# Sharing one pool between the operands of even head pairs and the first chunks' Gram operands, and loading the first of these during the operand stage

## The chip, the cores and the metric

The kernel runs on one core of one Trainium2 chip. The metric is the device time of one execution in microseconds (us); the lower the better. The kernel before was timed three times: 1175.95, 1177.39 and 1180.84 us, median 1177.39 us.

## The reference

A two-layer encoder trunk on x of 1024 positions by 1024 channels, float32. Layer 0: RMSNorm, one projection of 1024 to 4224 columns, mixer A (RWKV-7 time mixing, 8 heads of 64), mixer B (chunked attention, 8 heads of 64), gates, output projection, residual. Layer 1: RMSNorm, projection, gMLP spatial gating, output projection, residual; then a last RMSNorm. What matters here is mixer A's recurrence, which the kernel computes in chunks of 64 positions:

```
def step(state, inp):
    r_t, w_t, k_t, v_t, a_t, b_t = inp
    sa = einsum('bhvk,bhk->bhv', state, a_t)
    state = state * w_t + sa x b_t + v_t x k_t
    y_t = einsum('bhvk,bhk->bhv', state, r_t)
```

Here r, k and v are token-shifted slices of the projection, w the decay, a_t = -kk and b_t = kk * a.

## The kernel before

**Projections.** Every float32 matmul with the large weights is made as three fp32r products (high x high, high x low, low x high; lines 256, 258, 260). The tile they add into is named `acc`, and these matmuls are called acc matmuls below. 128 columns of weights are loaded by SyncE (`wraw`, line 221), split by ScalarE and GpSimd (`wh` line 222, `wl` line 225) and used in two halves of 24 acc matmuls.

**Operand stage** (lines 539 to 640). Four pairs of heads, `p` = 0 to 3, each with two halves of 512 positions. For each pair k, r and v are projected into the tiles `kT`, `rT`, `vT`, then `ar` (the a and r operands) and `bk` (the b and k operands) are formed and stored to DRAM: `ar_d` by line 604, `bk_d` by lines 535 and 537 in three stores. The function `bonus` stores v as `v_d` (line 626). `kT`, `rT` and `vT` are four halves each in the pools `rst` and `ra`, so that pairs p and p+2 use the same halves. These pools live on the left side of SBUF and are closed by `pi.close()` (line 640).

**Gram stage**, `stage_a(q)`, q = 0 to 3 (lines 667 to 728). A quarter has 4 chunks, taken in two chunk pairs `cg` = 0, 1. Per chunk pair SyncE loads `bk` (line 694, one load), `ag` (line 696, two loads, one for each head of a pair) and `uv` (line 699, four small loads). TensorE makes 16 Gram matmuls (line 713, `psg`; each shows as two instructions in the trace) in two groups of 8; VectorE masks each group out of PSUM into `G` and `ag` (line 717, four operations, with the mask `gmask` that GpSimd builds at line 656); GpSimd scales `bk` (line 678) and TensorE transposes it (line 684, `pst`). In the first quarter `bk` of cg 0 and both `ag` are tiles of the pool `re_`, which lies where `rst` and `ra` lay, and `bk` of cg 1 is a tile of `rb` on the right side.

**Inverse and recurrence.** `stage_b(q)` (line 730) inverts the unit triangular blocks: 30 short VectorE operations on `nq`, then ScalarE's `xe` (line 757), transposes to `dt`, and small matmuls `psx` (line 770). `stage_c(q)` (line 796) runs the four chunks in order, with matmuls `zz`, `yy`, `us` and copies `z`, `uv` between them; `zz` and `yy` of the first chunk stand among the Gram matmuls.

**Filling.** `Fill` hands out the acc matmuls of attention's projections between the small matmuls; their results leave by `split_evac` (`hl`, to `q_d` and `k_d`) and `vb_evac` (ScalarE's `vs`, line 893, then four transposes `pv`, line 896). The order on each engine is made by the Tile framework's scheduler from priorities and its own estimate of when each operand is ready; each engine then runs its row in order, and SyncE's row holds all DMA issues.

Of the kernel before, what the change touches and what calls it, by code (L numbers as in the profile page):

```python
# [8 lines left out]
F32 = mybir.dt.float32  # L9
# [9 lines left out]
P = 128  # L19
# [34 lines left out]
LATE = 1  # L54
NPO = 1
QP = 84
FILLS = [5, 4, 4, 6, 4, 3, 3, 3]
QA = 14
QB = [80, 10, 10, 10]
# [40 lines left out]
def trunk_kernel(  # L100
# [4 lines left out]
    nc = tc.nc  # L105
# [20 lines left out]
        (sg_ln_g.rearrange("a (r c) -> (a r) c", c=P), 8),  # L126
    ]
    nrow = sum(n for _, n in rows)
    pi = ExitStack()
    ca = pi.enter_context(tc.tile_pool(name="ca", bufs=1))  # L130
    rst = pi.enter_context(tc.tile_pool(name="rst", bufs=1, reuse_waits="tile"))
# [14 lines left out]
    o = 0  # L146
# [295 lines left out]
    def lora_evac(ps, hf):  # L442
# [5 lines left out]
            tc.add_manual_dep(i_.ins, evs[-1][0].ins.name, sched_only, reason="issue order")  # L448
        nc.vector.tensor_tensor(xw[64:128, sl], w, f32(xw[0:64, sl]), op=ALU.subtract)
        nc.vector.tensor_tensor(xa[0:64, sl], a, f32(xa[64:128, sl]), op=ALU.subtract)  # L450
    new_half = lambda tag: (rst if tag == "kT" else ra).tile([P, 512], F32, tag=tag, name=tag, bufs=4)
    kT = [new_half("kT") for _ in range(2)]
    sh_k = shifted(kT, 4)
    for hf in range(2):
        run(half_steps(w_lora, hf, lora_evac))
# [81 lines left out]
            nc.sync.dma_start(dst[64:128, :, 64 * i:64 * i + 64], src[64:128, :, 64 - 64 * i:128 - 64 * i])  # L537

    for p in range(NPAIR):
        rT, vT = ([new_half(tag) for _ in range(2)] for tag in ("rT", "vT"))  # L540
        if p > 0:
            kT = [new_half("kT") for _ in range(2)]
            proj_cm(w_in_e[0], 512 + p * P, shifted(kT, 4 + p))
        after = evs[AFW[0]][0] if p == 0 and AFW[0] else None
        proj_cm(w_in_e[0], p * P, shifted(rT, p), after=after)
# [118 lines left out]
    hss = [slice(64 * h, 64 * h + 64) for h in range(2)]  # L664
    oss = hss[::-1]

    def stage_a(q):

        d = quart[q]
        d["ag"], d["g"], d["bt"], d["uv"] = [], [], [], []  # L670
        rq = (re_, rb)[q % 2]
        parts = []

        def rest(cg, bk, bt):

            c0 = 4 * q + 2 * cg
            for i in range(2):
                nc.gpsimd.tensor_tensor(
                    bk[:, :, i, :], bk[:, :, i, :], pcs[:, c0 + i, :].unsqueeze(2).to_broadcast([P, 4, P]), op=ALU.mult)
            for pj in range(2):  # L680
                pst = ps_m.tile([P, 4, P], F32, tag="m", name="pst")
                for j in range(2):
                    for i in range(2):
                        nc.tensor.transpose(pst[:, 2 * j + i], bk[:, 2 * pj + j, i, :], ident)
                nc.scalar.copy(bt[:, 2 * pj:2 * pj + 2].rearrange("p j i t -> p (j i) t"), pst)

        for cg in range(2):
            o = 4 * q + 2 * cg
            uv = rq.tile([P, 2, 4, P], F32, tag="uv", name="uv", bufs=2)

            ag = rq.tile([P, 2, 4, 2, P], F32, tag="ag", name="ag", bufs=2)
            bk = (rb if q == 0 and cg else re_).tile(
                [P, 4, 2, P], F32, tag="bt" if q == 0 and cg else "bk", name="bk", bufs=2 if q == 0 and cg else 1)
            nc.sync.dma_start(bk, bk_d[o // 8][:, :, o % 8:o % 8 + 2, :].rearrange("a p c t -> p a c t"))
            for h in range(2):
                nc.sync.dma_start(ag[hss[h], h], ar_d[o // 8][:, hss[h], o % 8:o % 8 + 2, :].rearrange("a p c t -> p a c t"))
            for i in range(2):
                for h in range(2):
                    nc.sync.dma_start(
                        uv[oss[h], i, :, hss[h]],  # L700
                        v_d[o // 8][:, 64 * (o % 8 + i):64 * (o % 8 + i) + 64, hss[h]].rearrange("a s n -> s a n"))
                    if q == cg == i == 0:
                        nc.gpsimd.memset(uv[hss[h], i, :, hss[h]], 0.0)
            if cg == 0:
                d["G"] = rq.tile([P, 2, 4, 2, P], F32, tag="G", name="G", bufs=1)
            g = d["G"][:, cg]
            bt = rq.tile([P, 4, 2, P], F32, tag="bt", name="bt", bufs=2)
            for pj in range(2):
                psg = [ps_m.tile([P, 4, P], F32, tag="m", name=f"psg{h}") for h in range(2)]
                for j in range(2):  # L710
                    for i in range(2):
                        for h in range(2):
                            nc.tensor.matmul(psg[h][:, 2 * j + i], lhsT=bk[hss[h], 2 * pj + j, i, :],  # L713
                                             rhs=ag[hss[h], h, 2 * pj + j, i, :], start=True, stop=True)
                for h in range(2):
                    for dst, r in ((g[:, 2 * pj:2 * pj + 2], hss[h]), (ag[:, h, 2 * pj:2 * pj + 2], oss[h])):
                        nc.vector.tensor_tensor(
                            dst[r].rearrange("p j i t -> p (j i) t"), psg[h][r],
                            gmask[r].unsqueeze(1).to_broadcast([64, 4, P]), op=ALU.mult)
            d["g"].append(g)  # L720
            d["ag"].append(ag)
            d["bt"].append(bt)
            d["uv"].append(uv)
            parts.append((cg, bk, bt))
            if q > 0:
                rest(*parts.pop())
        for a in parts:
            rest(*a)
# [197 lines left out]
    for q in range(3):  # L926
# [4 lines left out]
        fill.pump(QB[q + 1], mark, FLB)  # L931
        stage_d(q)
    pe.close()


    pb = ExitStack()
# [450 lines left out]
```

## Time and profile before

| | |
|---|---|
| median of three runs | 1177.39 us (1175.95 to 1180.84) |
| profiled execution | 1180.27 us, of which the trace spans 1178.6 us |
| mean granted TensorE clock | 0.974 |
| TensorE busy | 1119.8 us, 95% of the span |
| VectorE, ScalarE, GpSimd busy | 53%, 40%, 37% |
| operand stage, Gram stage, recurrence | to about 265 us, from 269 us on, to about 545 us |

Engines are named as in the trace: PE = TensorE, PEld = its weight loads, DVE = VectorE, ACT = ScalarE, POOL = GpSimd, SP = SyncE. A timeline row gives the start, the time taken, engine, line, operation, tiles, count, and in square brackets the idle time ahead of it with what ended it. A row of the windows view gives the busy time and count of each engine in that stretch, then the clock granted to TensorE (1.00 is full), the busy share of the DMA engines and GB/s. All positions are us from the span's start.

### The profile page before, as it was taken

How to read it: one execution, taken by the hardware profiler on the slowest of the kernel's cores; microseconds unless marked ns; L12 is line 12 of the kernel's file. 1: busy time of each engine (PE TensorE's matmuls, PEld its weight loads, DVE VectorE, ACT ScalarE, POOL GpSimd, SP SyncE). 2: the span in 40 equal slices, each digit the busy share in tenths (PEclk: the TensorE clock that was granted, in tenths of full speed). 3: DMA queues.
4: the chain of work that ended last, by engine and by line, in shares of the span. 5: the costliest groups of instructions: out<-in, count | busy, mean ns of one | idle time of the engine just before them, and what ended most of it. 6: DMA issues, size and time to landing. Idle time of an engine off the chain costs nothing.

```text
span 1178.6 us, 21117 instructions
## 1 busy us (share of the span) xinstructions
PE 1119.8 (95%) x8162; PEld 929.2 (79%) x8162; DVE 622.6 (53%) x1276; ACT 469.0 (40%) x1008; POOL 432.0 (37%) x448
## 2 busy tenths in 40 slices
PE   8999999998899898999997899899999999999997
PEld 5788778787777676767886778789998888888886
DVE  6455656456585867634687767464100753333433
ACT  5554554430322232312675646234417232231432
POOL 4345545361223433423322463311402464351222
PEclk9999999995999998999999899999999999999999
DMA  6124446469322533293587784862401232122541
GB/s 209 39 81 143 116 117 164 140 205 193 109 83 83 161 101 100 73 215 118 162 227 184 222 264 147 270 216 90 134 10 55 87 110 72 63 88 89 166 133 71
DMA packets 169125, 156.39 MB, mean 133 GB/s; under 512 B 25257, under 2 KB 138562, under 8 KB 168898
## 3 DMA queue, kind: packets, MB, share of 16 engines
q1 hardware_dynamic: 169026, 155.06, 44.9%
q8 instruction: 64, 1.05, 0.4%
q14 instruction: 35, 0.29, 0.1%
HBM read 102.02 MB, written 53.00 MB: 132 GB/s over the span
## 4 chain that ended last, share of the span: by engine, by line
PE 58%; DMA 7%; DVE 5%; ACT 1%; issue 1%; POOL 1%; SPq 0%; DVEq 0%; ACTq 0%; POOLq 0%
PE acc L256 8%; PE acc L258 8%; PE acc L260 8%; PE accv L256 3%; PE accv L260 3%; PE accv L258 3%; PE accu L256 3%; PE accu L260 2%; PE accg L260 2%; PE accu L258 2%; PE accg L258 2%; PE accg L256 2%; PE st L1069 2%; DMA wraw<-in_w_out_e_dram 2%; PE psx L770 1%; PE psg L713 1%
## 5 line engine op out<-in xcount | busy, mean ns | idle before, releaser
L256 PE MATMUL acc<-xH,wh 128*128 128x512 f32 x528 | 214.7, 407 | 1.6 <-DVE rT L422 0.6
L258 PE MATMUL acc<-xL,wh 128*128 128x512 f32 x528 | 213.5, 405 | 0.0
L225 POOL TENSOR_TENSOR wl<-wraw,wh 128x512 fp32r<-128x512 f32 (+1 forms) x106 | 148.9, 1424 | 175.4 <-ACT wh L222 160.0
L260 PE MATMUL acc<-xH,wl 128*128 128x512 f32 x528 | 212.0, 401 | 0.0
L256 PEld LDWEIGHTS acc<-xH,wh 128*128 128x128 f32 x528 | 101.5, 192 | 23.6 <-DVE rT L422 1.0
L258 PEld LDWEIGHTS acc<-xL,wh 128*128 128x128 f32 x528 | 101.2, 192 | 21.2 <-issue 0.9
L260 PEld LDWEIGHTS acc<-xH,wl 128*128 128x128 f32 x528 | 101.0, 191 | 21.2
L256 PE MATMUL acc<-WHL,yh 128*128 128x512 f32 x256 | 101.9, 398 | 4.5 <-DVE res L1142 3.4
L222 ACT CAST wh<-wraw 128x512 fp32r<-128x512 f32 (+1 forms) x102 | 62.7, 653 | 108.5 <-PE acc L258 43.3
L258 PE MATMUL acc<-WHL,yh 128*128 128x512 f32 x256 | 100.8, 394 | 0.0
L260 PE MATMUL acc<-WHL,yl 128*128 128x512 f32 x256 | 100.8, 394 | 0.0
L256 PE MATMUL accv<-wh,xH 128*128 128x256 f32 x256 | 71.7, 283 | 0.0
L258 PE MATMUL accv<-wl,xH 128*128 128x256 f32 x256 | 71.7, 283 | 0.0
L260 PE MATMUL accv<-wh,xL 128*128 128x256 f32 x256 | 71.4, 285 | 0.0
L256 PEld LDWEIGHTS acc<-WHL,yh 128*128 128x128 f32 x256 | 48.4, 189 | 15.6 <-DVE res L1142 4.1
L258 PEld LDWEIGHTS acc<-WHL,yh 128*128 128x128 f32 x256 | 48.3, 189 | 9.6 <-POOL WHL L1114 0.2
L260 PEld LDWEIGHTS acc<-WHL,yl 128*128 128x128 f32 x256 | 48.1, 188 | 9.7
L256 PE MATMUL accu<-xH,wh 128*128 128x512 f32 x128 | 50.5, 395 | 0.0
L260 PE MATMUL accu<-xH,wl 128*128 128x512 f32 x128 | 49.9, 390 | 0.0
L258 PE MATMUL accu<-xL,wh 128*128 128x512 f32 x128 | 49.9, 390 | 0.0
L260 PE MATMUL accg<-xH,wl 128*128 128x512 f32 x128 | 49.9, 389 | 0.0
L256 PE MATMUL accg<-xH,wh 128*128 128x512 f32 x128 | 49.8, 389 | 0.0
(433 smaller groups left out, 2438.0 us busy)
## 6 DMA issues: line engine op xcount, KB each, us to landing
wraw<-in_w_in_e_dram SPq DMA_DIRECT2D x66, 256.0 KB
wraw<-in_w_in_o_dram SPq DMA_DIRECT2D x32, 256.0 KB
xt<-in_x_dram SPq DMA_DIRECT2D x8, 512.0 KB
ar_d<-ar SPq DMA_DIRECT2D x8, 512.0 KB
q_d<-hl SPq DMA_DIRECT2D x8, 512.0 KB
bk<-bk_d SPq DMA_DIRECT2D x8, 512.0 KB
ag<-ar_d SPq DMA_DIRECT2D x16, 256.0 KB
k_d<-hl SPq DMA_DIRECT2D x8, 512.0 KB
```

Of the source, the lines that this page charges most:

```text
L222: c_ = hi(wh[:, ks], raw)
L225: nc.gpsimd.tensor_tensor(wl[:, ks], raw, f32(wh[:, ks]), op=ALU.subtract)
L256: fill(nc.tensor.matmul(ps, lhsT=ah(k), rhs=bh(k), start=(k == 0), stop=False), k == 0)
L258: fill(nc.tensor.matmul(ps, lhsT=ah(k), rhs=bl(k), start=False, stop=False), False)
L260: fill(nc.tensor.matmul(ps, lhsT=al(k), rhs=bh(k), start=False, stop=(k == nk - 1)), False)
L713: nc.tensor.matmul(psg[h][:, 2 * j + i], lhsT=bk[hss[h], 2 * pj + j, i, :], rhs=ag[hss[h], h, 2 * pj + j, i, :], start=True, stop=True)
L770: nc.tensor.matmul(ps[t_, i], lhsT=lhsT(f, i), rhs=rhs[f[0], i], start=True, stop=True)
L1069: nc.tensor.transpose(st[:, o:o + P], pfs[j][:, k0:k0 + P], ident)
```

## The change

A new pool `eo` is opened ahead of the operand stage's pools and closed after the last `stage_d` of the loop. It has two tiles: `e4` of 4 KB and `e8` of 8 KB for each partition. `kT` of pairs 0 and 2 is now one `e4` tile, `rT` and `vT` of these pairs one `e8` tile; odd pairs keep `rst` and `ra`, with two halves of each kind where there were four. `ag` of the first chunk pair of quarters 0 and 2 is an `e8` tile, and every `bk` but that of quarter 0's second chunk pair is an `e4` tile. The first chunk pair's `bk` and `ag` loads get a priority 1000 steps higher.

```
+FIRST = 1000
+    es = ExitStack()
+    eo = es.enter_context(tc.tile_pool(name="eo", bufs=1, reuse_waits="tile"))
...
-    new_half = lambda tag: (rst if tag == "kT" else ra).tile([P, 512], F32, tag=tag, name=tag, bufs=4)
-    kT = [new_half("kT") for _ in range(2)]
+    def operands(p):
+
+        if p % 2:
+            return ([(rst if tag == "kT" else ra).tile([P, 512], F32, tag=tag, name=tag, bufs=2) for _ in range(2)]
+                    for tag in ("kT", "rT", "vT"))
+        k_ = eo.tile([P, 2, 512], F32, tag="e4", name="kT", bufs=1)
+        rv = eo.tile([P, 4, 512], F32, tag="e8", name="rvT", bufs=1)
+        return ([t_[:, i] for i in range(o, o + 2)] for t_, o in ((k_, 0), (rv, 0), (rv, 2)))
+
+    kT, rT, vT = operands(0)
...
     for p in range(NPAIR):
-        rT, vT = ([new_half(tag) for _ in range(2)] for tag in ("rT", "vT"))
         if p > 0:
-            kT = [new_half("kT") for _ in range(2)]
+            kT, rT, vT = operands(p)
...
-            ag = rq.tile([P, 2, 4, 2, P], F32, tag="ag", name="ag", bufs=2)
-            bk = (rb if q == 0 and cg else re_).tile(
-                [P, 4, 2, P], F32, tag="bt" if q == 0 and cg else "bk", name="bk", bufs=2 if q == 0 and cg else 1)
-            nc.sync.dma_start(bk, bk_d[o // 8][:, :, o % 8:o % 8 + 2, :].rearrange("a p c t -> p a c t"))
-            for h in range(2):
-                nc.sync.dma_start(ag[hss[h], h], ar_d[o // 8][:, hss[h], o % 8:o % 8 + 2, :].rearrange("a p c t -> p a c t"))
+            ap_, at_, ab_ = (eo, "e8", 1) if q % 2 == cg == 0 else (rq, "ag", 1 + q % 2)
+            ag = ap_.tile([P, 2, 4, 2, P], F32, tag=at_, name="ag", bufs=ab_)
+            bp_, bt_, bb_ = (rb, "bt", 2) if q == 0 and cg else (eo, "e4", 1)
+            bk = bp_.tile([P, 4, 2, P], F32, tag=bt_, name="bk", bufs=bb_)
+            with tc.high_priority(offset=FIRST if q == cg == 0 else 0):
+                nc.sync.dma_start(bk, bk_d[o // 8][:, :, o % 8:o % 8 + 2, :].rearrange("a p c t -> p a c t"))
+                for h in range(2):
+                    nc.sync.dma_start(
+                        ag[hss[h], h], ar_d[o // 8][:, hss[h], o % 8:o % 8 + 2, :].rearrange("a p c t -> p a c t"))
```

How the rows of the engines move is shown at three places. First SyncE's row before, from the stores of the last pair's first half on (line 604 stores `ar`, 537 and 535 store `bk`, 221 loads weights, 432 stores a gate):

```order
L604 DMA ar_d_109<-ar 128x1024
L432 DMA bg_d<-gt 128x512
L537 DMA bk_d_111<-bk 512x1x64
L535 DMA bk_d_111<-bk 64x1024
L537 DMA bk_d_111<-bk 512x1x64
L221 DMA wraw<-in_w_in_e_dram 128x4x128
L432 DMA bg_d<-gt 128x512
```

The same place in the change, where the numbers of lines and of DRAM tiles are a few higher (616 is 604, 548 and 550 are 535 and 537, 225 is 221; 710 and 708 load `ag` and `bk`):

```order
L616 DMA ar_d_112<-ar 128x1024
L436 DMA bg_d<-gt 128x512
L710 DMA ag<-ar_d_112 64x4x256 x2
L548 DMA bk_d_114<-bk 64x1024
L550 DMA bk_d_114<-bk 512x1x64 x2
L225 DMA wraw<-in_w_in_e_dram 128x4x128
L708 DMA bk<-bk_d_114 128x4x256
L436 DMA bg_d<-gt 128x512
```

The first chunk pair's three loads now stand behind the stores they read. Further on in SyncE's row, at the end of the operand stage, stood before:

```order
L221 DMA wraw<-in_w_in_e_dram 128x4x128
L694 DMA bk<-bk_d_111 128x4x256
L696 DMA ag<-ar_d_109 64x4x256 x2
L699 DMA uv<-v_d_113 64x4x64 x4
L694 DMA bk<-bk_d_111 128x4x256
L696 DMA ag<-ar_d_109 64x4x256 x2
```

and stands in the change (714 loads `uv`):

```order
L225 DMA wraw<-in_w_in_e_dram 128x4x128
L714 DMA uv<-v_d_116 64x4x64 x4
L708 DMA bk<-bk_d_114 128x4x256
L714 DMA uv<-v_d_116 64x4x64 x2
L710 DMA ag<-ar_d_112 64x4x256 x2
```

The second chunk pair's `ag` has seven small or large loads ahead of it since the weights, and had eight. Second, TensorE's row before, at the end of the last acc matmuls ahead of the Gram stage:

```order
L258 MATMUL acc<-xL,wh 128x512
L260 MATMUL acc<-xH,wl 128x512
L713 MATMUL psg_2566<-ag,bk 128x128 x4
L713 MATMUL psg_2567<-ag,bk 128x128 x4
L713 MATMUL psg_2580<-ag,bk 128x128 x4
L814 MATMUL zz<-uv,ag 64x64
L817 MATMUL yy<-uv,ag 64x64
L713 MATMUL psg_2581<-ag,bk 128x128 x4
```

and in the change (728 is 713), nineteen acc matmuls earlier:

```order
L260 MATMUL acc<-xH,wh 128x512
L262 MATMUL acc<-xL,wh 128x512
L728 MATMUL psg_2561<-ag,bk 128x128 x2
L728 MATMUL psg_2562<-ag,bk 128x128 x2
L728 MATMUL psg_2561<-ag,bk 128x128
L728 MATMUL psg_2562<-ag,bk 128x128
L728 MATMUL psg_2561<-ag,bk 128x128
L728 MATMUL psg_2562<-ag,bk 128x128
L264 MATMUL acc<-xH,wl 128x512
```

The first group of 8 has moved ahead of the last nineteen acc matmuls; the second group (now `psg_2575` and `psg_2576`) and the second chunk pair follow these, in the order they had. Third, ScalarE's row before, after the Gram stage (685 copies the transposed `bk`, 222 splits weights, 884 is the `hl` copy, 757 `xe`, 893 `vs`, 898 the copy of `pv`):

```order
L884 ACTIVATE hl<-acc 128x512
L685 COPY bt<-pst 128x512 x2
L757 ACTIVATE xe<-nq,half 128x16x16 x2
L893 ACTIVATE vs<-acc 128x512
L898 CAST vv<-pv 128x8x64
L222 CAST wh<-wraw 128x512 x2
```

and in the change (697 is 685, 772 is 757, 908 is 893, 913 is 898):

```order
L899 ACTIVATE hl<-acc 128x512
L697 COPY bt<-pst 128x512 x2
L908 ACTIVATE vs<-acc 128x512
L913 CAST vv<-pv 128x8x64
L772 ACTIVATE xe<-nq,half 128x16x16 x2
L226 CAST wh<-wraw 128x512 x2
```

`vs` and the copy of its transposes have changed places with `xe`. From here to the end of `stage_c(2)` the rows of TensorE, VectorE, ScalarE and GpSimd stand in another order at many places, with the same operations; from `stage_c(3)` on they stand almost as before.

More of the change, by code (lines that the diff above doesn't have):

```diff
@@ L933, in trunk_kernel @@
     pe.close()
+    es.close()
     pb = ExitStack()
```

## The prediction

> **What bounds the kernel now.** I read the page first: how much of the span TensorE is busy, and at what clock.
>
> ```profile
> PE 1119.8 (95%) x8162; PEld 929.2 (79%) x8162; DVE 622.6 (53%) x1276; ACT 469.0 (40%) x1008; POOL 432.0 (37%) x448
> ...
> PEclk9999999995999998999999899999999999999999
> ```
>
> TensorE is the bound: 95% busy, no other engine over 53%. So a change can win in two ways only: less idle time of TensorE, or a fuller clock while it is busy. The tenth slice of the clock shows 5 where the others show 8 or 9, and it lies at 265 to 295 us, where the Gram stage begins. So I took the windows view there, cut at the places where TensorE's work changes, and once over the stretch of inverse and recurrence.
>
> ```profile
> 265.40:269.20 3.80, 0.01 (x1) 0.00 (x0) 0.00 (x0) 0.00 (x0) 0.00 (x0) 1.00 1.15 257
> 269.20:285.70 16.50, 16.45 (x96) 14.68 (x96) 9.53 (x15) 0.00 (x0) 2.37 (x3) 0.53 1.16 215
> 285.70:288.80 3.10, 1.85 (x9) 1.47 (x9) 3.02 (x4) 0.59 (x1) 1.71 (x2) 0.50 0.61 175
> 288.80:294.00 5.20, 5.20 (x14) 4.12 (x13) 4.70 (x12) 0.65 (x2) 0.00 (x0) 0.50 0.31 101
> 300.60:304.00 3.40, 1.21 (x18) 1.01 (x18) 2.12 (x9) 1.39 (x3) 0.45 (x2) 1.00 0.57 172
> 304.00:307.70 3.70, 3.70 (x12) 3.03 (x13) 3.61 (x6) 0.59 (x1) 0.00 (x0) 0.54 0.01 2
> 330.00:545.00 215.00, 199.33 (x2996) 156.06 (x2995) 135.47 (x296) 60.13 (x127) 75.97 (x88) 0.96 0.44 121
> ```
>
> The first row is a hole of 3.8 us. In the next three rows, 25 us in all, TensorE is busy, but at half its clock. Then the same once more in small: a hole in 300.6 to 304.0, half clock behind it. The timeline of TensorE says what ends the holes.
>
> ```profile
> 264.79 0.39 PE L258 MATMUL acc<-xL,wh 128*128 128x512 f32 x1
> 265.02 0.39 PE L260 MATMUL acc<-xH,wl 128*128 128x512 f32 x1
> 269.25 4.93 PE L713 MATMUL psg<-ag,bk 64*128 64x128 f32 x24 [3.85 <-DMA ag<-ar_d]
> 277.37 2.07 PE L713 MATMUL psg<-ag,bk 64*128 64x128 f32 x8
> 282.62 3.09 PE L713 MATMUL psg<-ag,bk 64*128 64x128 f32 x16
> 300.55 1.17 PE L713 MATMUL psg<-ag,bk 64*128 64x128 f32 x16
> 303.91 0.82 PE L896 MATMUL pv<-ident,vs 128*128 128x128 f32 x4 [2.19 <-ACT vs L893]
> 378.65 1.16 PE L713 MATMUL psg<-ag,bk 64*128 64x128 f32 x8
> ```
>
> Acc matmuls start 0.23 us apart (first two rows). The first hole is ended by the load of `ag`, the second by ScalarE's `vs`. Gram matmuls at half clock take 2.07 us for 8 instructions; at full clock 1.16 us, or 1.17 us for 16 where the heads alternate. The first chunk pair runs from 269.25 to 277.37, the second from there to 285.71 (282.62 + 3.09), 8.3 us. Last, the issues of SyncE:
>
> ```profile
> 229.42 0.32 SPq L604 DMA_DIRECT2D ar_d<-ar  x1
> 233.74 0.52 SPq L537 DMA_DIRECT2D bk_d<-bk  x1
> 238.94 0.38 SPq L221 DMA_DIRECT2D wraw<-in_w_in_e_dram  x1
> 261.71 1.28 SPq L694 DMA_DIRECT2D bk<-bk_d  x1
> 263.04 1.37 SPq L696 DMA_DIRECT2D ag<-ar_d  x2
> 264.51 2.55 SPq L699 DMA_DIRECT2D uv<-v_d  x4
> 267.11 0.60 SPq L694 DMA_DIRECT2D bk<-bk_d  x1
> ```
>
> The first pair's data was stored from 229.4 and 233.7 us on, but its loads are issued at 261.7 to 264.4; the last lands 4.8 us after its issue.
>
> **Part by part.** I follow the new order with these durations, in the profiled execution's own time (1180.27 us, span 1178.6).
>
> *The early loads and the first group.* In the change the three loads stand behind the stores, so they land some 15 us before their use. The first 8 Gram matmuls come nineteen acc matmuls earlier: at 265.4 - 19 x 0.23 = 261.1 us. They take 1.2 us, and the nineteen acc matmuls end at 266.6 where they ended at 265.4: so the first group costs no wait. Its masking on VectorE needs `gmask`, and takes four operations:
>
> ```profile
> 261.66 0.92 POOL L656 TENSOR_SCALAR_AFFINE_SELECT gmask<-gmask 64x64 f32<-64x64 f32 x4
> ...
> L717 DVE TENSOR_TENSOR ag<-psg,gmask 64x512 f32<-64x512 f32 x7 | 4.8, 689 | 0.1
> ```
>
> From 262.6 these are 4 x 0.69 = 2.8 us, done at 265.4, under the acc matmuls. The second group with four `zz` and four `yy` follows at full clock: twice 1.16 us and about 0.7 us, so the first chunk pair is done at 269.6 instead of 277.4.
>
> *The second chunk pair* is now the one that is waited for. Its `ag` loads have seven issues ahead of them since the weights: from 261.7 four `uv` (2.55), `bk` (0.6), two `uv` (1.3) and itself (1.4) make 267.5. With the 4.8 us from issue to landing seen above that is 272.3; with nothing queued ahead I estimate 2 us, 269.5 (0.5 MB at the 257 GB/s of the first row above). I take 271.5, nearer the first, since the DMA share was over 1.0 there and one load of 0.5 MB less lies ahead. At half clock (next paragraph) its 8.3 us end at 279.8, where they ended at 285.7: **5.9 us gained**. Bounds: 7.8 if nothing is waited for (269.6), 3.3 if the data lands at 274.1.
>
> *The clock.* Two windows of 3.4 us, and what followed them:
>
> ```profile
> 266.73:270.14 3.41, 0.89 (x8) 0.92 (x8) 0.00 (x0) 0.00 (x0) 0.00 (x0) 1.00 1.24 206
> 270.14:294.03 23.89, 22.64 (x111) 19.35 (x110) 17.28 (x29) 1.26 (x3) 4.08 (x4) 0.50 0.89 186
> 300.86:304.27 3.41, 1.22 (x19) 1.02 (x16) 2.17 (x8) 1.39 (x3) 0.45 (x2) 1.00 0.49 144
> ```
>
> Both windows that TensorE filled to about a third (0.89 and 1.22 of 3.41 us) are followed by half clock, the second though its hole was 2.2 us. The long row shows that Gram matmuls on 64 rows don't bring the clock back though TensorE reads busy; it came back after 5.2 us of acc matmuls. In the change a wait of about 2 us stands between 3 us of Gram matmuls and more of them, so I expect half clock again, from about 270 to the acc matmuls' fifth us: no gain in this but what lies above. *The transposes and the acc matmuls behind* keep 3.1 and 5.2 us.
>
> *`vs` ahead of `xe`.* Before, ScalarE held `vs` behind `xe`, which waited for the inverse's loop:
>
> ```profile
> 302.47 0.91 ACT L757 ACTIVATE xe<-nq,half 128x256 f32<-128x256 f32 x2 [5.54 <-DVE nq L754]
> 303.29 0.58 ACT L893 ACTIVATE vs<-acc 128x512 f32<-128x512 f32 x1
> ...
> 305.73 0.71 DVE L762 STREAM_TRANSPOSE dt<-D 128x512 f32<-128x512 f32 x1
> ```
>
> Now `vs` runs when its acc matmuls end, under the 1.2 us of Gram matmuls that follow, and the hole of 2.2 us goes; with it the half-clock window, 3.4 us at half speed, 1.7 us: **3.9 us gained**, bounds 0 (another hole takes its place) and 3.9. What is late next is `dt`: before, the inverse was done 20.7 us after the last Gram matmul (285.7 to 306.4), now at 279.8 + 20.7 + 2 for the maskings now ahead of it = 302.5; TensorE reaches its `psx` at about 302.9. It just holds.
>
> *New short waits.* TensorE comes to the second quarter's transposes 1.5 us (one acc matmul, one `psx` set) after its Gram matmuls, and GpSimd's scaling between them takes 2.0 us:
>
> ```profile
> 276.26 2.04 POOL L678 TENSOR_TENSOR bk<-bk,pcs 128x512 f32<-128x512 f32 x2 [11.25 <-PE psg L713]
> ```
>
> That is 0.6 us; with `psx` sets that have less work between them than before I take **1.6 us lost**, bounds 0 and 3.
>
> *Moved past on SyncE.* Behind the early loads wait three `bk` stores, two weight loads and the stores of a gate and of v. The load of `ag` waits for a store issued 4 us before it, so it holds the row about 1 us; that of `bk` waits for stores issued at 234 to 236, so it may hold the weight load of 238.94 by 2 us. Weights hardly ended a wait from 225 to 300 us (total, times, longest):
>
> ```profile
> ACT wh L222 <- DMA wraw<-in_w_in_e_dram: 0.9, 1, 0.9
> ```
>
> I cost it at nothing. The odd pairs' halves and `eo`'s tiles are reused two pairs on, as before: nothing.
>
> *Inverse and recurrence, 330 to 545 us.* The order is dealt anew. Of 215 us TensorE idles 15.7, and a clock of 0.96 costs 8.6 more. The longest waits there are mostly single ones (total, times, longest):
>
> ```profile
> PE us L830 <- DVE uv L827: 3.1, 4, 1.2
> PE psg L713 <- DMA bk<-bk_d: 2.7, 1, 2.7
> PE psy L871 <- DVE G L789: 2.4, 1, 2.4
> PE yy L837 <- ACT uv L827: 1.9, 1, 1.9
> ...
> 362.71 0.57 PE L814 MATMUL zz<-uv,ag 128*64 128x64 f32 x12 [1.88 <-issue]
> ```
>
> A wait of some 2.3 us with its half-clock window (1.7) is 4 us; one such pair more or less is likely, which way I can't tell: 0, with 5 either side.
>
> **The sum**: -5.9 - 3.9 + 1.6 = -8.2 us. The profiled execution would become 1172.1; it lies 2.9 above the median of the three runs, so for the median I say 1177.4 - 8.2 = **1169.2 us**.
>
> **The rivals.** *A: the clock stays up.* If the shortened wait no longer drops the clock, the second chunk pair is bound by VectorE (8 x 0.69 = 5.5 us instead of 8.3) and twelve acc matmuls take 2.7 us instead of 5.2: 5.3 us more, 1163.9 us. The Trainium skill, "TensorE: Matmul & The Clock Gate", Part 1, says the clock halves after an idle window of about 3.4 us. By it a wait of 2 us would leave the clock alone, and the time would be this rival's. The trace speaks against it: 2.2 us at 303.91 were enough. For it: 1.9 us at another place (`zz`, 362.71) were not. *B: given back.* The stretch to 545 us follows the chain of inverse and recurrence; then only what the Gram stage's end gains counts, less the new waits, and one more pair of wait and low window (4) takes the rest: -5.9 + 1.6 + 4 = -0.3, 1177.1 us. For it: VectorE is busy 63% there and its row has changed most. Against it: TensorE still works 93% of that time. *C: slower.* In the new row of VectorE the second quarter's inverse stands among the first recurrence's copies. Waits for the copy `uv` were 3.1 us in four times, 0.8 each, the longest 1.2. If each of twelve more steps waited that 1.2, it would cost 14.4: 1177.4 - 8.2 + 14.4 = 1183.6 us. It is slower than before from 0.7 us a step on; before, the copies stood among the same loop without it. *D: no earlier.* The order shows the loads moved, so that the change does nothing is no case; that the second pair's data is as late as it can be is the bound of 3.3 above (1171.8), and lies in the forecast.
>
> **How the numbers follow.** About 0.5%, 5.9 us, is what a measurement can tell here. Forecast 0.53 (0.44 of it beyond 5.9 us, 0.09 within); A 0.12; B 0.27 (0.03 beyond, 0.24 within); C 0.08. So faster 0.59, same 0.33, slower 0.08. The range goes down to the forecast less 5 for the dealt order and 3 for part of A, 1161, and up past B to 1179; 2 in 10 stay outside, most of C and the far half of A.
>
> **What would show it.** Right: eight Gram matmuls among the acc matmuls before 265 us with no wait; a hole of 1 to 4 us ahead of the second chunk pair, ended by `ag` or `bk`; half clock from about 270 to 288; the last Gram matmul of quarter 0 near 280; no hole at `pv`. Wrong: a hole over 5 us at the second pair; full clock through the Gram stage (A); Gram stage earlier but `stage_c(3)` not (B); VectorE's `uv` ending more waits of TensorE than before (C); weight loads ending waits before 265 us.

## The result, and the profile after

The change takes 1172.55 us (median of seven runs, 1168.48 to 1174.72), the kernel before 1178.65 us beside it (seven runs). The ratio is 0.9934, with a 95% interval of 0.9912 to 0.9957: 7.8 us less (5.1 to 10.4). The profiled execution took 1174.60 us, at the upper end of its runs; its trace spans 1172.9 us at a mean clock of 0.973.

The page of the changed kernel, at the two lines that were shown of before:

```profile
PE 1120.8 (96%) x8162; PEld 928.9 (79%) x8162; DVE 622.2 (53%) x1276; ACT 468.9 (40%) x1008; POOL 432.8 (37%) x448
...
PEclk8999999997979999999998999999999999999999
```

TensorE's work is the same. The tenth slice of the clock, 5 before, is 7 now; the twelfth, 322 to 352 us, has fallen from 9 to 7. So the loss of clock was made smaller in one place and came up in another. To see how much, I cut both traces into four stretches, from the Gram stage to the first attention score. I reckon TensorE's loss in a stretch from its row of the windows view as two parts: the length less PE busy (idle), and the length times what the clock lacks to 1.00. The first block is the kernel before, the second the change (length, busy time of each engine, clock, DMA share, GB/s):

```profile
265.40:310.00 44.60, 37.31 (x187) 31.38 (x187) 29.83 (x60) 5.86 (x11) 7.05 (x8) 0.69 0.70 154
310.00:360.00 50.00, 47.01 (x980) 37.38 (x981) 33.25 (x69) 15.73 (x32) 14.74 (x18) 1.00 0.32 98
360.00:450.00 90.00, 81.97 (x1302) 64.97 (x1289) 63.71 (x135) 26.54 (x54) 31.83 (x37) 0.97 0.41 113
450.00:549.00 99.00, 93.45 (x1238) 72.75 (x1237) 51.16 (x110) 27.20 (x58) 38.96 (x43) 0.94 0.49 133
```

```profile
265.40:310.00 44.60, 41.17 (x442) 33.85 (x443) 32.33 (x65) 9.96 (x18) 13.17 (x16) 0.85 0.64 155
310.00:360.00 50.00, 42.17 (x758) 34.30 (x747) 28.30 (x64) 12.53 (x26) 9.90 (x14) 0.80 0.24 71
360.00:450.00 90.00, 85.40 (x1306) 67.33 (x1299) 65.19 (x136) 27.63 (x57) 34.99 (x38) 1.00 0.42 121
450.00:541.80 91.80, 88.45 (x1204) 69.05 (x1203) 51.33 (x111) 25.14 (x54) 36.60 (x41) 0.98 0.53 141
```

| TensorE's loss, us (idle + clock) | before | change | difference |
|---|---|---|---|
| 265.4 to 310 | 7.3 + 13.8 = 21.1 | 3.4 + 6.7 = 10.1 | -11.0 |
| 310 to 360 | 3.0 + 0 = 3.0 | 7.8 + 10.0 = 17.8 | +14.8 |
| 360 to 450 | 8.0 + 2.7 = 10.7 | 4.6 + 0 = 4.6 | -6.1 |
| 450 to the first attention score | 5.6 + 5.9 = 11.5 | 3.4 + 1.8 = 5.2 | -6.3 |
| sum | 46.3 | 37.7 | -8.6 |

The first attention score comes 7.3 us earlier (541.76 where it was 549.04). The Gram stage gave what it was to give; then more than all of it was lost in the next 50 us, and won back up to 542. The timeline of TensorE shows the places. In the kernel before, the first Gram matmuls stood at 269.25 behind a hole of 3.85 us, the last one of quarter 0 ended at 285.71, `pv` came at 303.91 behind 2.19 us, and `psx` at 311.78:

```profile
261.67 1.17 PE L728 MATMUL psg<-ag,bk 64*128 64x128 f32 x16
272.44 1.74 PE L728 MATMUL psg<-ag,bk 64*128 64x128 f32 x8 [2.13 <-DMA ag<-ar_d]
277.36 3.09 PE L728 MATMUL psg<-ag,bk 64*128 64x128 f32 x16
295.61 0.66 PE L911 MATMUL pv<-ident,vs 128*128 128x128 f32 x4
303.31 1.29 PE L785 MATMUL psx<-dt,G 32*32 32x32 f32 x128
316.62 1.81 PE L728 MATMUL psg<-ag,bk 64*128 64x128 f32 x16 [2.47 <-DMA bk<-bk_d]
329.96 1.11 PE L839 MATMUL us<-z,G 64*64 64x64 f32 x14 [2.51 <-DVE G L804]
349.79 0.50 PE L852 MATMUL yy<-uv,G 64*64 64x64 f32 x10 [2.85 <-issue]
448.60 0.69 PE L845 MATMUL us<-uv,bt 128*64 128x64 f32 x16 [2.58 <-DVE uv L842]
541.76 0.22 PE L1021 MATMUL sc<-T1k,T2q 128*128 128x128 f32 x1
```

The first chunk pair has no wait. The second waits 2.13 us for `ag`, runs at half clock and ends at 280.45. There is no hole at `pv`. New up to 360 us are three holes: of 2.47 us at 316.6, ended by the load of `bk`, of 2.51 us at 330.0, ended by VectorE's copy `G`, and of 2.85 us at 349.8, in which TensorE waited for nothing that the profile shows ("issue"). SyncE issues the early loads where the order has them:

```profile
232.77 1.28 SPq L710 DMA_DIRECT2D ag<-ar_d  x2
238.92 0.40 SPq L708 DMA_DIRECT2D bk<-bk_d  x1
267.61 1.27 SPq L710 DMA_DIRECT2D ag<-ar_d  x2
```

Their waits held up little: the last weight load of the operand stage, at 261.23 before, is issued at 261.75 now. The loads move because their tiles are free, and hardly by the priority: with `FIRST` at 0 the order of the engines differs in SyncE's row alone, where one load of `ag` and that of `bk` stand a few places further back (that order was not run).

### The profile page after: what moved, and what is told of

The parts are those of the page before. It is cut to its first block, busy times and chain, and to the rows that moved or that the text cites. A ratio compares the mean times of both kernels' runs of the same rounds, so it can differ in the third digit from the quotient of the medians.

```text
span 1172.9 us, 21112 instructions
## 1 busy us (share of the span) xinstructions
PE 1120.8 (96%) x8162; PEld 928.9 (79%) x8162; DVE 622.2 (53%) x1276; ACT 468.9 (40%) x1008; POOL 432.8 (37%) x448
## 4 chain that ended last, share of the span: by engine, by line
PE 78%; DMA 9%; DVE 7%; ACT 2%; SPq 2%; issue 2%; POOL 1%; DVEq 0%; POOLq 0%; ACTq 0%
PE acc L262 13%; PE acc L264 13%; PE acc L260 13%; PE accv L260 3%; PE accv L264 3%; PE accv L262 3%; PE accu L260 3%; PE accu L264 2%; PE accg L264 2%; PE accu L262 2%; PE accg L262 2%; PE accg L260 2%; PE psg L728 2%; PE st L1085 2%; DMA wraw<-in_w_out_e_dram 1%
## 5 line engine op out<-in xcount | busy, mean ns | idle before, releaser
L260 PE MATMUL acc<-xH,wh 128*128 128x512 f32 x528 | 211.7, 401 | 1.3 <-ACT xH L305 0.7
L264 PEld LDWEIGHTS acc<-WHL,yl 128*128 128x128 f32 x256 | 48.5, 189 | 10.7 <-POOL yl L1143 0.9
L260 PE MATMUL accu<-xH,wh 128*128 128x512 f32 x128 | 50.5, 395 | 0.0
```

What stands on the lines that cost most here:

```text
L260: fill(nc.tensor.matmul(ps, lhsT=ah(k), rhs=bh(k), start=(k == 0), stop=False), k == 0)
L264: fill(nc.tensor.matmul(ps, lhsT=al(k), rhs=bh(k), start=False, stop=(k == nk - 1)), False)
```

## The experiments

All were timed against the kernel before, which took 1177.6 to 1180.2 us (medians) beside them; so they are compared by their ratios to it. The change itself stands at 0.9934. The loss is that of the table above, in its four stretches, each from that kernel's own windows rows up to its own first attention score.

| run | edit | ratio (95%) | loss by stretch, us | sum |
|---|---|---|---|---|
| the change | | 0.9934 (0.9912 to 0.9957) | 10.1, 17.8, 4.6, 5.2 | 37.7 |
| late_loads | early loads late again | 1.0024 (0.9998 to 1.0050) | 19.4, 15.4, 2.0, 13.7 | 50.5 |
| xe_first | `vs` behind `xe` again | 0.9988 (0.9965 to 1.0010) | 15.6, 9.0, 2.9, 17.6 | 45.1 |
| xe_first_norm | the same, normalisation later | 0.9966 (0.9946 to 0.9986) | 15.5, 9.6, 2.0, 15.8 | 42.9 |
| own_bk | second tile for `bk` | 0.9933 (0.9911 to 0.9956) | 11.1, 10.2, 3.7, 15.8 | 40.8 |
| own_bg | the same, `bg` early | 0.9869 (0.9838 to 0.9900) | 11.7, 11.1, 2.4, 10.0 | 35.2 |
| bg_two | two buffers for `bg` | 0.9916 (0.9888 to 0.9944) | 10.4, 12.0, 4.7, 3.8 | 30.9 |
| uv_last | second pair's loads ahead of `uv` | 0.9936 (0.9910 to 0.9961) | 10.9, 14.4, 5.5, 4.0 | 34.8 |
| fill_hole | acc matmuls in the hole | 0.9926 (0.9899 to 0.9953) | 8.0, 13.7, 6.4, 10.6 | 38.7 |
| fill_own | the same and own_bk | 0.9908 (0.9874 to 0.9942) | 6.2, 14.4, 6.9, 8.6 | 36.1 |
| before_fill | before, hole filled | 0.9989 (0.9965 to 1.0012) | 10.4, 14.6, 2.0, 19.7 | 46.7 |
| before_fill_norm | the same, normalisation later | 0.9976 (0.9953 to 1.0000) | 14.6, 12.0, 2.0, 14.6 | 43.2 |
| all_four | fill, own tile, `bg`, normalisation | 0.9853 (0.9821 to 0.9885) | 7.7, 13.9, 5.3, 4.7 | 31.6 |

The loss is of one execution, the ratio of many, and the two need not rank runs alike: `bg_two` has the smallest sum, in an execution 2.7 us under its median, and own_bk's trace is of its slowest. Single waits differ by 2 us between traces that have the same order there (own_bk, below).

### The early loads undone

```
-            with tc.high_priority(offset=FIRST if q == cg == 0 else 0):
+            def load(after=None):
...
+            if q or cg:
+                load()
             for i in range(2):
                 for h in range(2):
-                    nc.sync.dma_start(
+                    u_ = nc.sync.dma_start(
...
+                    if q == cg == i == h == 0:
+                        load(u_)
```

> The change with its shared tiles, but the three loads of the first chunk pair are issued behind the first uv load, at about 262 us, where they stood before; vs stays ahead of xe. My account (the Gram stage's end counts, 5.3 us of it): the first Gram matmuls wait some 4 to 5 us for ag, half clock runs from about 270 us for some 24 us, the last Gram matmul of quarter 0 ends near 286, and the time is 4 to 7 us above the change's 1172.6, 1176.5 to 1179.5. Rival (the gain comes from the order dealt behind the Gram stage, not from the loads): within 2 us of the change, 1170.5 to 1174.5, though the hole is back.

Measured: 1.0024, 0.9% above the change (some 10.6 us). The Gram stage of late_loads, TensorE's rows and the windows row:

```profile
271.22 3.18 PE L735 MATMUL psg<-ag,bk 64*128 64x128 f32 x16 [5.54 <-DMA ag<-ar_d]
285.40 3.09 PE L735 MATMUL psg<-ag,bk 64*128 64x128 f32 x16
```

```profile
265.40:310.00 44.60, 37.28 (x202) 31.33 (x202) 28.58 (x59) 6.80 (x13) 8.51 (x13) 0.73 0.70 153
```

The hole is 5.5 us, the last Gram matmul of quarter 0 ends at 288.49, 8.0 us later than in the change (two of these are because one `uv` load now stands ahead, so that the data is later than it was before). The stretch to 310 loses 7.3 + 12.0 = 19.4 us, 9.3 more than the change. The recurrence has sixteen steps, one for each chunk, counted here from 0. It runs 5.8 to 5.9 us behind the change's for steps 2 to 8, less at some of the steps after them (3.4 at step 9) and 5.3 at step 14, so what the Gram stage loses does arrive. The first attention score comes 10.4 us later (552.2): the other 5.1 us go in the last step, where GpSimd waits for the gates `bg` with a small operation of the step, `Sp`, behind it:

```profile
529.08 1.27 POOL L897 TENSOR_TENSOR cen<-cen,bg 128x512 f32<-128x512 f32 x1 [13.87 <-DMA bg<-bg_d]
```

From the `us` of step 14 to that of step 15 it is 17.8 us here, 15.3 in the kernel before, 12.7 in the change, and 11.3 in own_bg and bg_two (below), where GpSimd has no such wait. The rival, that the loads don't count, falls. The 4 to 7 us that I had expected are what the recurrence shows up to step 14; the rest of the 10.6 is the wait for `bg`, which I had not foreseen.

### `vs` behind `xe` again

```
-            nc.scalar.activation(xe[:, :, 16 * x_:16 * x_ + 16], nq, AF.Copy, scale=half[:, x_:x_ + 1])
+            d["xe"] = nc.scalar.activation(xe[:, :, 16 * x_:16 * x_ + 16], nq, AF.Copy, scale=half[:, x_:x_ + 1])
...
-            nc.scalar.activation(vs, ps, AF.Copy, scale=0.5)
+            vs_ = nc.scalar.activation(vs, ps, AF.Copy, scale=0.5)
+            if p == hf == 0:
+                tc.add_manual_dep(vs_.ins, quart[0]["xe"].ins.name, sched_only, reason="issue order")
```

> The change with the first vs put behind xe on ScalarE, as before; the loads stay early. My account (the vs term, 3.9 us): in the change xe ran at 300.3 to 301.2 us, so vs ends near 301.8 and TensorE, done with its Gram matmuls by 296 to 297, waits 2 to 5 us at pv; a half-clock window follows; the time is 4 to 7 us above the change's 1172.6, 1176.5 to 1179.5. Rival (the inverse and the recurrence behind it are the chain, and TensorE's hole at pv is slack): under 2 us above, 1172.5 to 1174.5.

Measured: 0.9988, 0.54% above the change, 6.4 us. The number is as expected, the place only in part. ScalarE and TensorE of xe_first:

```profile
298.53 0.91 ACT L772 ACTIVATE xe<-nq,half 128x256 f32<-128x256 f32 x2 [7.61 <-DVE nq L769]
299.35 0.57 ACT L908 ACTIVATE vs<-acc 128x512 f32<-128x512 f32 x1
```

```profile
296.96 3.57 PE L728 MATMUL psg<-ag,bk 64*128 64x128 f32 x16 [1.61 <-DVE ag L732]
```

The scheduler put a second group of Gram matmuls ahead of `pv`, and these waited 1.6 us for VectorE's masking; 6.8 us of half clock follow. The stretch to 310 loses 15.6 us, 5.5 more than in the change: that is the `vs` term. But 310 to 450 loses less than in the change, and 450 to the first score 12 us more. Three waits make most of that, of which the longest is this one, on VectorE and on TensorE:

```profile
493.78 1.21 DVE L874 TENSOR_REDUCE vr<-yt 128x16 f32<-128x1024 f32 x1
502.61 0.70 DVE L804 COPY xs<-psx 32x512 f32<-32x512 f32 x1
```

```profile
503.37 1.92 PE L785 MATMUL psx<-D,xs 32*32 32x32 f32 x64 [4.06 <-DVE xs L804]
```

Quarter 2's normalisation, from its second reduction on, stood on VectorE ahead of the last quarter's `xs`; in the change it stands behind it. So I put it there by hand:

```
-                    (nc.vector.tensor_copy if k else nc.scalar.copy)((xs[rs_] if o is None else g[rs_, :, o:o + 32]), ps[rs_])
+                    d["inv"] = (nc.vector.tensor_copy if k else nc.scalar.copy)((xs[rs_] if o is None else g[rs_, :, o:o + 32]), ps[rs_])
...
-        nc.vector.reduce_sum(vr, yt.rearrange("p a (h n) -> p (a h) n", n=64), axis=AX.X)
+        vr_ = nc.vector.reduce_sum(vr, yt.rearrange("p a (h n) -> p (a h) n", n=64), axis=AX.X)
+        if q == 2:
+            tc.add_manual_dep(vr_.ins, quart[3]["inv"].ins.name, sched_only, reason="issue order")
```

> xe_first again (the first vs behind xe), with the normalisation of quarter 2 (from its second reduction on) put behind the last quarter's inverse on VectorE. In xe_first some 9 us of normalisation stood between the second dt and the copy xs, TensorE waited 4.1 us for xs, and the time lost against the change appeared only from 470 us on; up to step 11 xe_first was 3.5 us ahead. If that order on VectorE is what xe_first lost: 4 to 8 us under xe_first, the change's time or less, 0.4 to 1.0% under the kernel before. If vs behind xe is what it lost: within 2 us of xe_first, 0.0 to 0.3% under the kernel before.

Measured: 0.9966, 0.22% under xe_first, 2.6 us, between the two expectations; the intervals overlap. The wait for `xs` fell to 1.4 us, the other two stayed:

```profile
475.02 0.69 PE L845 MATMUL us<-uv,bt 128*64 128x64 f32 x16 [3.21 <-DVE uv L842]
494.75 0.45 PE L829 MATMUL zz<-uv,ag 128*64 128x64 f32 x8 [1.98 <-issue]
504.10 1.20 PE L785 MATMUL psx<-D,xs 32*32 32x32 f32 x64 [1.41 <-DVE xs L804]
```

So the order of the normalisation explains that one wait; what it is worth in time is not shown. What the one dependency on ScalarE did to the last quarter isn't told apart further.

### The hole at 316.6: a tile of its own for `bk`, and `bg`

```
-            bp_, bt_, bb_ = (rb, "bt", 2) if q == 0 and cg else (eo, "e4", 1)
+            bp_, bt_, bb_ = (rb, "bt", 2) if q == 0 and cg else (re_, "bk1", 1) if cg else (eo, "e4", 1)
...
-        dt = re_.tile([P, 16, 32], F32, tag="dt", name="dt", bufs=2)
+        dt = re_.tile([P, 16, 32], F32, tag="dt", name="dt", bufs=1)
```

`dt` gets one buffer at both of its places; that makes the room.

> The change with a tile of its own for bk of every second chunk pair from quarter 1 on, so that this load needn't wait for the transposes of the first chunk pair's bk; the room comes from dt, one buffer for two. My account of what was given back: the hole of 2.5 us at 316.6, ended by that bk load, and the 17.1 us of half clock behind it go; TensorE is the bound, so 2.5 us and most of the half of 17.1 us come back, 4 to 9 us off the change's 1172.6, 1163.5 to 1168.5. Rival (the recurrence's chain sets the time there, TensorE's lost clock is slack): within 2 us, 1170.5 to 1174.5. Half clock can also come at another place: then the stretch at half clock is as long as in the change but starts later.

Measured: 0.9933, the change's own ratio, as the rival had it, but not for its reason. The hole at 316.6 is gone and the stretch from 310 to 360 loses 10.2 us in place of 17.8. Not all of that is the tile's doing: in bg_two and uv_last `bk` has the tile that it has in the change, its load is issued at 309.26 and 308.82 us (308.88 in the change), and TensorE waits 0 and 0.31 us for it; these stretches lose 12.0 and 14.4. So the 2.47 us in the change's trace are a load that landed some 2 us later after its issue than in those two. But 450 to the first score now loses 15.8 in place of 5.2. TensorE and GpSimd of own_bk at that place:

```profile
523.82 0.47 PE L852 MATMUL yy<-uv,G 64*64 64x64 f32 x2 [4.60 <-ACT uv L842]
```

```profile
520.20 1.26 POOL L890 TENSOR_TENSOR cen<-cen,bg 128x512 f32<-128x512 f32 x1 [15.69 <-DMA bg<-bg_d]
521.54 1.26 POOL L891 TENSOR_TENSOR cen<-cen,bg 128x512 f32<-128x512 f32 x1
522.76 1.29 POOL L825 TENSOR_TENSOR Sp<-uv,pcs 64x256 f32<-64x256 f32 x2
```

GpSimd waits 15.7 us for `bg`, the gates; `Sp` of the next step stands behind that in its row, the copy `uv` waits for `Sp`, and TensorE for `uv`. The last step takes 18.6 us. The load of `bg` is issued at 510.77, behind attention's loads, and takes 9.4 us to land. `bg` has one buffer. Two kernels take that wait away. One loads quarter 2's second `bg` into the tile that own_bk gave to `bk`:

```
-            bg = rb.tile([P, 4, 2, P], F32, tag="bg", name="bg", bufs=1)
+            ob = q == 2 and a == 1
+            bg = (re_ if ob else rb).tile([P, 4, 2, P], F32, tag="bk1" if ob else "bg", name="bg", bufs=1)
```

> own_bk again, and the second bg of quarter 2 loaded into that tile of bk's, free by then, so that its load goes ahead of attention's loads. own_bk was 5 to 7 us ahead of the change up to step 14 and then lost 6 us, where GpSimd waited 15.7 us for bg with Sp behind it. If that wait is where own_bk's gain went: the recurrence stays 5 to 7 us ahead, and the time is 3 to 7 us under own_bk's, 0.9 to 1.3% under the kernel before. If the gain is lost at the next wait in its place, or attention's loads now wait for that tile: within 2 us of own_bk, 0.5 to 0.8% under the kernel before.

Measured: 0.9869 (0.9838 to 0.9900), 0.64% under own_bk, 7.5 us (a little over the 3 to 7 expected), and outside the change's interval. GpSimd of own_bg, where the wait for `bg` is gone and `Sp` comes when the step before is done:

```profile
504.77 1.28 POOL L891 TENSOR_TENSOR cen<-cen,bg 128x512 f32<-128x512 f32 x1
...
521.25 1.29 POOL L825 TENSOR_TENSOR Sp<-uv,pcs 64x256 f32<-64x256 f32 x2 [4.88 <-DVE uv L850]
```

Up to step 14 the two run alike (4.8 and 5.0 us ahead of the change); the last step takes 11.3 us in place of 18.6, and that is the difference. So it is shown that own_bk lost its gain at the wait for `bg`. The other kernel is the change with only a second buffer for `bg` (`bufs=2` there and `bufs=1` for `dt`):

> The change with two buffers for bg, the gates that GpSimd multiplies in at the end of a quarter, so that the second load of a quarter goes ahead of attention's loads; the room comes from dt, one buffer for two. In the change GpSimd waits 12.9 us for bg at 509.9 to 522.8 and the Sp behind it, which the step's uv copies wait for, holds TensorE for 1.3 us at 525. My account: the wait for bg goes, step 14 to 15 shortens by 1 to 2 us, the time is 0 to 3 us under the change's, 8 to 11 us under the kernel before. Rival (the order is dealt anew and what is gained there is lost elsewhere): within 2 us of the change either way.

Measured: 0.9916, 0.18% under the change, 2 us; as expected, and not to be told from no difference. Its interval overlaps own_bg's too, so what `bk`'s own tile brings beside an early `bg` is not shown.

### The wait for the second chunk pair

First the place of its loads, `offset=FIRST if q == 0 else 0` for `offset=FIRST if q == cg == 0 else 0`:

> The change with bk and ag of quarter 0's second chunk pair issued ahead of all uv loads, at about 262 to 265 us in place of 265.7 to 268.9. If a short hole alone drops the clock (my account: two windows with a third of TensorE's work in them were followed by half clock), the hole of 2.1 us at 272.4 shrinks or goes and with it the half clock of 13.7 us: 2 to 7 us off the change's 1172.6, 1165.5 to 1170.5. If the second chunk pair's data is bound by the transfers and not by its place in the row, or the first zz and yy wait for the uv loads in its place: the hole stands elsewhere, within 2 us of 1172.6. Rival: Gram matmuls with 64 rows drop the clock by themselves, hole or none: half clock from about 270 us on all the same, and only the hole's 2 us gained.

Measured: 0.9936, no difference. The hole moved to the first `zz`, which now waits for `uv`, and the same 13.7 us of half clock follow:

```profile
271.56 0.24 PE L829 MATMUL zz<-uv,ag 128*64 128x64 f32 x1 [2.86 <-DMA uv<-v_d]
```

Then work in the hole, with two constants:

```
-QP = 84
+QP = 102
...
-QB = [80, 10, 10, 10]
+QB = [62, 10, 10, 10]
```

> The change with eighteen acc matmuls (4.1 us of work) taken from behind the Gram stage and put ahead of its second chunk pair, where TensorE waited 2.1 us for ag. The hole goes. My account (a hole in the window drops the clock): with it go the 13.7 us of half clock behind it, the last Gram matmul of quarter 0 ends near 279 to 280 in spite of 4.1 us more work ahead of it, and the time is 3 to 7 us under the change's, that is 11 to 15 us under the kernel before. Rival (Gram matmuls on 64 rows drop the clock by themselves, hole or none): half clock from about 275 on for 14 us all the same; only the hole's 2 us are gained, 8 to 11 us under the kernel before. Second rival (the inverse, which now starts later, is the chain): no gain, 6 to 9 us under the kernel before.

Measured: 0.9926, not told from the change. But the clock answers what the experiment asked. The first block is the change's hole and what follows it, the second the same place in fill_hole, where Gram matmuls, `zz`, `yy` and ten of the acc matmuls stand without a hole:

```profile
269.60:272.40 2.80, 0.70 (x14) 0.44 (x13) 1.62 (x3) 0.00 (x0) 2.04 (x2) 1.00 1.10 217
272.80:286.50 13.70, 12.45 (x62) 10.52 (x62) 9.93 (x13) 1.17 (x2) 2.04 (x2) 0.50 0.76 138
```

```profile
267.90:278.00 10.10, 9.86 (x91) 8.13 (x90) 7.55 (x12) 1.64 (x3) 4.89 (x5) 1.00 1.07 198
```

With no hole the Gram matmuls run at full clock to the end, 277.8 us, 2.7 us earlier than in the change though 4.1 us of work stand ahead of them. So the hole drops the clock, and the rival, that Gram matmuls on 64 rows do it by themselves, falls. What is gained goes at the next places:

```profile
295.80 3.35 PE L728 MATMUL psg<-ag,bk 64*128 64x128 f32 x16 [3.24 <-DVE ag L732]
...
499.13 1.11 PE L886 MATMUL psy<-ident,cen 128*128 128x128 f32 x4 [5.34 <-DVE G L804]
```

The masking behind the inverse's loop ends the first. The second is ended by the copy `G`, ahead of which the normalisation stands on VectorE, as it stood ahead of `xs` in xe_first; one of its operations (line 73) took 3.08 us in fill_hole and 0.13 in xe_first. The same with own_bk's tile:

> The eighteen acc matmuls ahead of the second chunk pair, and a tile of its own for bk of every second chunk pair from quarter 1 on, together. With the latter alone the recurrence ran 5 to 7 us earlier up to step 14, and then waited 4.6 us in one place for Sp behind GpSimd's wait for bg, so that nothing was left. My account: the recurrence comes 5 to 12 us earlier than in the change up to step 14, and gives 4 to 7 us of that back at the same wait for bg; 9 to 14 us under the kernel before. Rival (what is gained ahead of attention is never lost there): as much as fill_hole and 5 us more.

Measured: 0.9908, 10.9 us under the kernel before, as expected; its interval still overlaps the change's. The place is not as expected: it gives some 4 us back at step 12, with a wait of 2.10 us for `G` at 496.3 and half clock behind it, and its last step takes 11.9 us.

### The kernel before with its hole filled

The same two constants in the kernel before:

> The kernel before, without the change, with eighteen acc matmuls (4.1 us) taken from behind the Gram stage and put ahead of it, where TensorE waited 3.85 us for ag. If what the early loads bring is no more than that the hole has work in it, this has it too: the hole goes, perhaps with the 23.9 us of half clock behind it; the hole at pv may stay. 3.9 us and up to 8 more under the kernel before: 1166 to 1174 where that is 1177.6. Rival (the Gram stage's end counts for the inverse and the recurrence, and here it comes no earlier): within 2 us of the kernel before.

Measured: 0.9989, no gain. The stretch to 310 loses 10.4 us, as little as in the change, without the early loads; so what the change gains in that stretch can be had with two constants. But 310 to 360 loses 14.6 and 450 to the first score 19.7. Two of its holes follow. The first, in the stretch from 265, is ended by the load of `bk`, which SyncE reaches behind two weight loads and one of `bg`, issues at 286.71 without a wait for its tile, and which lands some 6.5 us later; the second by the normalisation ahead of `xs`:

```profile
293.26 3.06 PE L713 MATMUL psg<-ag,bk 64*128 64x128 f32 x16 [3.59 <-DMA bk<-bk_d]
...
505.90 1.92 PE L770 MATMUL psx<-D,xs 32*32 32x32 f32 x64 [4.07 <-DVE xs L789]
```

With the normalisation behind the inverse, by the same dependency as above:

> The kernel before without the change, with the eighteen acc matmuls ahead of the Gram stage (before_fill) and the same order on VectorE: normalisation of quarter 2 behind the last quarter's inverse. before_fill was level with the change up to step 11 and lost 8 us from 470 us on by the same three waits as xe_first. If the early loads bring no more than a hole filled: about the change's time, 0.4 to 1.0% under the kernel before. Rival (without the early loads the time comes back elsewhere): within 0.2% of the kernel before.

Measured: 0.9976, 0.13% under before_fill: neither expectation. The loss there fell from 19.7 to 14.6, and in this execution the Gram stage had a hole and half clock again (14.6 for 10.4). The interval of before_fill lies above the change's, that of before_fill_norm just touches it (0.9953 and 0.9957). So a filled hole without the early loads is likely not the change's equal; which part of the rest is the order alone stays open.

### All four

The eighteen acc matmuls, own_bk's tile, `bg` in it, and the normalisation behind the inverse:

> The change with all four: eighteen acc matmuls ahead of the second chunk pair, bk's own tile, bg's early load in it, the normalisation of quarter 2 behind the last quarter's inverse. Each alone removes a wait at another place (272, 317, 523 and 503 us). My account (TensorE is the bound at each of these places, and what one place gains the next no longer takes): 6 to 12 us under the change, 1.2 to 1.7% under the kernel before. Rival (the chain of the recurrence gives a limit that fill_own has reached): as fill_own, 0.8 to 1.0% under the kernel before.

Measured: 0.9853 (0.9821 to 0.9885), 1163.05 us beside 1180.22: 17.3 us under the kernel before and 9.6 under the change by the ratios, as my account had it. Its windows rows:

```profile
265.40:310.00 44.60, 41.80 (x363) 34.10 (x362) 30.31 (x65) 9.65 (x18) 13.05 (x16) 0.89 0.76 187
310.00:360.00 50.00, 43.10 (x957) 34.95 (x957) 29.79 (x67) 14.23 (x29) 9.88 (x14) 0.86 0.22 65
360.00:450.00 90.00, 86.54 (x1197) 68.42 (x1195) 69.05 (x143) 26.91 (x56) 36.20 (x41) 0.98 0.41 116
450.00:535.20 85.20, 82.16 (x1163) 65.03 (x1163) 44.67 (x100) 24.55 (x52) 32.56 (x37) 0.98 0.53 143
```

The largest loss left is 13.9 us from 310 to 360. It beats both kernels; against own_bg its interval doesn't separate it.

## Why the prediction was right, point by point

**The total** was forecast at -8.2 us, and by the ratio -7.8 were measured (the two medians lie 6.1 apart). Two of its terms hold; the other two missed by more than their bounds, in opposite directions.

**The Gram stage's end** was put 5.9 us earlier. It came at 280.45 for 285.71, 5.3 us, in a trace that stood 0.5 us later up to there. The step holds in its parts: no wait at the first chunk pair, the second pair's data at 272.4 (forecast 271.5), half clock again. That it counts for the time is shown by late_loads, whose recurrence still runs 5.3 us later at step 14.

**`vs` ahead of `xe`** was put at 3.9 us, and what is late next, `dt`, was to just hold at 302.9. The hole and its half-clock window are gone; `dt` was done at 303.03 and `psx` came at 303.31 without a wait. With the Gram stage this makes 9.8 us forecast for the stretch to 310, and 11.0 measured. Undone one at a time the loads cost 9.3 us in that stretch and `vs` 5.5: more than 11.0 together, since each undone alone changes the order too.

**New short waits** were put at 1.6 us, with 3 as the bound. This step failed. The prediction's next term begins at 330 us; cut there, by the same reckoning, 310 to 330 lost 11.4 us where it had lost 0.9, 10.5 more. I had looked at the second quarter's transposes and `psx` sets. What came late was the load of `bk` behind these transposes, which needs their tile: 2.47 us of hole, and 17.1 us of half clock (317.1 to 334.2) in which the stretch has few acc matmuls to end it; then the wait for `G`. A wait for `bk` stood among the quoted rows, at 2.7 us, but at another place. That the load landed so late belongs to this trace (own_bk, above).

**The order dealt anew**, 0 with 5 either side, brought -7.9 us from 330 us to the first attention score (24.2 lost before, 16.3 now, with the clock unrounded), and -12.4 from 360 us on: the second failed step. From 360 us on the kernel before had four holes of 1.9 to 2.7 us, ended by `bk`, `G`, `uv` and issue, and 17.1 us of half clock; the change has one hole of that size, 2.6 us at 448.6, and 3.4 us of half clock. 2.6 us of the gain lie in the last step alone, 12.7 us where it took 15.3, by how long it waits behind `bg`. That the two misses cancel is partly luck: kernels with another order there (xe_first, before_fill) lost 12 to 15 us more than the change from 450 us on.

**Rival A**, the clock stays up: it fell for the change, and its mechanism was shown by fill_hole, where there is no hole. The rule of the Trainium skill that it weighed, "TensorE: Matmul & The Clock Gate", Part 1, asks for an idle window of about 3.4 us; here a hole of 2.13 us sufficed, so the measurement decides against it. Its price, 5.3 us, didn't reach the end of fill_hole either (0.08% under the change). **Rival B**, given back: true from 310 to 360, and undone after. **Rival C**, the copies `uv` behind the inverse: from 330 to 545 us VectorE's `uv` ended five of TensorE's waits, 4.6 us in all and the longest 2.6, where it had ended four, 3.1 us. Its sign came, but at 1.5 us and not at 14.4. **D** was no case.

## What to carry to other kernels

Where a scheduler deals the order anew, reckon TensorE's loss by stretch, idle time and clock together, up to a place that all kernels share; a stage that ends earlier is no gain until the next waits let it through. Look in advance for the tiles with one buffer whose load waits for another engine (here `bk` and `bg`), and for what stands behind that wait in a row: own_bk alone brought nothing, and with `bg` loaded earlier 7.5 us. That wait for `bg` made the last step 11.3 to 18.6 us long over these fourteen traces, so look where a difference arises before putting it down to an edit elsewhere. A short hole costs its half-clock window too; work put there saved that window in fill_hole, though the time was lost again at the next waits.

## What the runs showed of the hardware

The clock of these fourteen traces changes only on a grid of 3.41 us. From 230 to 1150 us it dropped 94 times. I sorted the windows of that grid at full clock by the share in which the records have TensorE busy: of 51 windows under 0.45 every one was followed by half clock, of 84 from 0.45 to 0.65 there were 33, of 3442 above there were 10. The clock came back 94 times, each time after a window busy for 0.89 or more, 84 times for 0.97 or more. At half clock two windows of the change that Gram matmuls on 64 rows fill throughout, with `zz` and `yy` between them (272.77 to 279.59 us), didn't bring it back, while at full clock such a window kept it (274.4 to 277.8 us in fill_hole, busy for 0.98).

VectorE's short operations were held beside GpSimd's. In xe_first, one operation of the inverse's loop and GpSimd's beside it:

```profile
466.72 1.29 DVE L769 TENSOR_TENSOR nq<-nq,nbt 128x15 f32<-128x15 f32 x1
468.26 0.19 DVE L769 TENSOR_TENSOR nq<-nq,nbt 128x28 f32<-128x28 f32 x1
```

```profile
466.70 1.27 POOL L891 TENSOR_TENSOR cen<-cen,bg 128x512 f32<-128x512 f32 x1
```

The operation that starts with GpSimd's ends with it, 1.29 us for one that takes 0.2; two more took 1.16 and 1.19 us beside `wl`, at 468.72 and 469.91. The 3.08 us of line 73 in fill_hole fell beside `wl` and a memset of GpSimd too. These delays in xe_first stand ahead of the copy `uv` for which TensorE waited 3.22 us there. That this made the wait was not tried.
